# RWKV-7 chunk products: the order of the two heads of a pair on TensorE

## The chip, the cores and the metric

The kernel runs on one core of a Trainium2 chip. The metric is the device time of one execution in microseconds; the median of the runs shown for the kernel before is 1680.67 us.

## The reference

The program is one hybrid layer (sparse attention beside RWKV-7) followed by a differential-attention layer and a gated-linear-attention layer, each with a convolutional feed-forward block, on 512 tokens of width 1024 in f32. The change touches only the RWKV-7 mixer of the first layer. It has 8 heads of 64 and carries a 64x64 state per head over all tokens:

```python
def rwkv7_step(state, inp):
    r_t, w_t, k_t, v_t, kk_t, a_t = inp
    sa = jnp.einsum('bhvk,bhk->bhv', state, -kk_t)
    state = (state * w_t[:, :, None, :] + sa[..., None] * (kk_t * a_t)[:, :, None, :]
             + v_t[..., None] * k_t[:, :, None, :])
    y = jnp.einsum('bhvk,bhk->bhv', state, r_t)
    return state, y
```

Around it stand the projection with a token shift, the decays and gates, a group norm of y per head, a bonus term, a silu gate and the output projection. The kernel computes the recurrence in chunks of 64 tokens: products within a chunk, the inverse of a triangular 64x64 matrix per chunk and head, and a short chain of states over the 8 chunks.

## The kernel before, in words

Tensors are kept with features on the partitions, or with tokens on the partitions in four blocks `tb` of 128 (`NT` = 4). A block of 128 tokens holds two chunks, so `c` = 0, 1 chooses the partitions `cr` = 64c to 64c + 63. A pair of heads `f` (four pairs) shares 128 feature partitions; `hp` = 0, 1 is the head in the pair and `rows` its half, 64hp to 64hp + 63. A product `mm(out, lhsT, rhs)` on TensorE reads both operands from the same partitions (rows of the array) and writes the partitions of `out` (columns of the array). So a 64x64 product uses a quarter of the array: the row half is given by the operands' partitions, the column half by the output's.

The first phase (`phase_a`, up to some 490 us) mixes two lines of work by a written list of steps (`ORDER`): the sparse attention (steps C, K, P0 to P3, G) and the RWKV mixer. The latter is `rwkv_s1` for each pair f (steps A0 to A3), then `rwkv_inv` (I: the triangular inverses, mainly on VectorE), `rwkv_s2` (M: the six products with the inverse applied), `rwkv_chain` (H: the states over 8 chunks) and `rwkv_s5` (F: norm and gate). After both, the output projection `w_o0`. The steps are Python generators; each `yield` is where the next step of the list comes in. Weights come by DMA (`wahead`), ScalarE makes an f16 high part (`whi`) and VectorE the rest (`wlo`, line 374), always two blocks ahead, in the order of a plan.

The program is written with a tile library: it tracks which instruction reads and writes which tile, sets all waits, and writes the order in which each engine runs its instructions, with the order of the program as priority. PSUM banks have tags. The RWKV products of this phase have one bank, tag "x" (line 458, `psx()`); a product into a new `psx` tile waits until the one before it has been read. Phase A's other banks are p (2), s (3), g (1) and o (1).

The lines that matter:

- Lines 827 to 838 (`rwkv_s1`): products of 64 rows by 128 columns of output; the partitions `rows` of the head are read, and `c` chooses the column half. In the trace: `psx<-ar,sq`, `psx<-ar,sH`. Line 785, `psx<-c_u_inc,ld`: products over all 128 partitions.
- Lines 842 to 846: `psx<-sG,kT`. Here `c` chooses row half and column half together.
- Lines 848 to 861: the products that the change reorders in `rwkv_s1`, `psx<-kT,sG` and `psx<-sG,acc`. For each c, one bank takes 16 products: for the first head four blocks tb of two, then the same for the second head. ScalarE then copies the bank into Y and KV.
- Lines 946 to 970 (`rwkv_s2`): for each pair and c, 32 products into two tiles `p` and `p2`: `psx<-x,AX` (into pv; LR lies in the tile x), `psx<-Bh,AX` and `psx<-AX,Bh` (into pv2). Again first head, then second head. VectorE adds pv into R and Y, adds pv2 into KV, and makes four tiles of GT (tile lx).
- The inversion's tiles (`lx`, lines 867 to 878) come from a pool that is opened after the pool of `rwkv_s1` is closed.

Of the kernel before, what the change touches and what calls it, by code (L numbers as in the profile page):

```python
# [18 lines left out]
NT = 4  # L19
# [206 lines left out]
class Kern:  # L226
# [521 lines left out]
    def rwkv_s1(self, f):  # L748
# [51 lines left out]
        bh, kh = W("D"), W("E")  # L800
# [11 lines left out]
        khT, vT = (W(l).rearrange("p (b c) -> p b c", b=NT) for l in "AG")  # L812
        dst = [P["AX"][:, 2 * f:2 * f + 2, :, 0:64], P["Bh"][:, :, fc], khT, vT]
        for src, d, kind in ((ar[:, 0, :], dst[0], 0), (bh, dst[1], 1), (kh, dst[2], 1), (v, dst[3], 1)):
# [3 lines left out]
            if kind == 0:  # L818
                pv = p.rearrange("p (b h k) -> p b h k", b=NT, h=2)
# [6 lines left out]
        kT = self.T(sp, [128, 2, NT, 2, 64], F32, "kT")  # L826
        for hp in range(2):
            rows = slice(64 * hp, 64 * hp + 64)
# [13 lines left out]
        for hp in range(2):  # L842
            for tb in range(NT):
                for c in range(2):
                    cr = slice(64 * c, 64 * c + 64)
                    self.mm(pxv[cr, hp, tb, :], kT[cr, hp, tb, 0, :], vT[cr, tb, 64 * hp:64 * hp + 64])
        self.act(P["AX"][:, 2 * f:2 * f + 2, :, 64:128], pxv, AF.Copy)
        for c in range(2):
            cr = slice(64 * c, 64 * c + 64)
            p = self.psx()  # L850
            pv = p.rearrange("p (a b v) -> p a b v", a=2, b=NT)
            for hp in range(2):
                rows = slice(64 * hp, 64 * hp + 64)
                for tb in range(NT):
                    vv = vT[cr, tb, 64 * hp:64 * hp + 64]
                    self.mm(pv[rows, 0, tb, :], vv, kT[cr, hp, tb, 1, :])
                    self.mm(pv[rows, 1, tb, :], khT[cr, tb, 64 * hp:64 * hp + 64], vv)
            yv = P["Y"][:, f, :].rearrange("p (b c t) -> p b c t", b=NT, c=2)
            self.act(yv[:, :, c, :], pv[:, 0], AF.Copy)
            kv = P["KV"][:, f].rearrange("p (b c) v -> p b c v", b=NT)  # L860
            self.act(kv[:, :, c, :], pv[:, 1], AF.Copy)
# [66 lines left out]
    def rwkv_s2(self):  # L928
        nc, ip = self.nc, self.tp
        P, LR, Tt = self.rwt, self.rwt["LR"], self.Tt  # L930
        AXu = P["AX"].rearrange("p h b n -> p (h b) n")
        for g in range(8):
            p = self.psx()
            pv = p.rearrange("p (u n) -> p u n", u=4)
            for u in range(4):
                for c in range(2):
                    cr = slice(64 * c, 64 * c + 64)
                    self.mm(pv[cr, u, :], Tt[cr, g * 4 + u, :], AXu[cr, g * 4 + u, :])
            self.act(AXu[:, g * 4:g * 4 + 4, :], pv, AF.Copy, scale=-1.0)
            if g % 4 == 3:  # L940
                yield
        WU = P["AX"]
        id64 = self.const("id64", ip)
        GT = self.T(ip, [128, 2, 32, 32], F32, "lx").rearrange("p a b c -> p (a b c)").rearrange("p (f n k) -> p f n k", f=4, n=8)
        R, Y, KV, Bh = P["R"], P["Y"], P["KV"], P["Bh"]
        for f in range(4):
            for c in range(2):
                cr = slice(64 * c, 64 * c + 64)
                p = self.psx()
                pv = p.rearrange("p (a b t) -> p a b t", a=2, b=NT)  # L950
                p2 = self.psx()
                pv2 = p2.rearrange("p (a b t) -> p a b t", a=2, b=NT)
                for hp in range(2):
                    rows = slice(64 * hp, 64 * hp + 64)
                    h = 2 * f + hp
                    for tb in range(NT):
                        rb = LR[cr, h, tb, 1, :]
                        bh = Bh[cr, tb, h * 64:h * 64 + 64]
                        self.mm(pv[rows, 0, tb, :], WU[cr, h, tb, 0:64], rb)
                        self.mm(pv[rows, 1, tb, :], WU[cr, h, tb, 64:128], rb)  # L960
                        self.mm(pv2[rows, 0, tb, :], WU[cr, h, tb, 0:64], bh)
                        self.mm(pv2[rows, 1, tb, :], bh, WU[cr, h, tb, 64:128])
                for dst, a in ((R, 0), (Y, 1)):
                    dv = dst[:, f, :].rearrange("p (b c t) -> p b c t", b=NT, c=2)[:, :, c, :]
                    self.tt(dv, dv, pv[:, a], ALU.add)
                kv = KV[:, f].rearrange("p (b c) v -> p b c v", b=NT)[:, :, c, :]
                self.tt(kv, kv, pv2[:, 1], ALU.add)
                for tb in range(NT):
                    n = tb * 2 + c
                    self.stt(GT[:, f, n, :], id64, P["egc"][:, f, n:n + 1], pv2[:, 0, tb, :], op1=ALU.add)  # L970
            if f < 3:
                yield
        self.GT = GT
# [980 lines left out]
```

## Time and profile before

| | us |
|---|---|
| median of 3 runs | 1680.67 (1676.7 to 1681.82) |
| the profiled execution | 1679.89 |
| its span, first to last instruction | 1678.1 |
| TensorE (PE) busy | 1595.4 |
| VectorE (DVE) busy | 1040.2 |
| ScalarE (ACT) busy | 756.3 |
| GpSimd (POOL) busy | 236.5 |

The profile is of one execution. Engines: PE is TensorE's matmuls, PEld its weight loads, DVE is VectorE, ACT is ScalarE, POOL is GpSimd. A row of a group names line (often a helper's: 298 is every matmul, 285 and 288 are VectorE's helpers), engine, operation and tiles as out<-in. "x32" counts instructions. The timeline merges neighbouring instructions of one group into a row with the first start and the time to the last end; a matmul's time there holds its whole passage, so rows overlap. Waits name the engine and the work that ended them.

### The profile page before, as it was taken

The numbers are of one execution on the slowest core, as the hardware profiler recorded it, in microseconds if no ns is written. First come the engines' busy times: TensorE is split into PE (matmuls) and PEld (weight loads), VectorE is DVE, ScalarE is ACT, GpSimd is POOL, SyncE is SP. The second block draws the span as 40 slices with busy tenths as digits, with TensorE's granted clock in tenths as the row PEclk, the third lists the DMA queues.
The fourth block names the chain that finished last, engine by engine and source line by source line (L and its number), as shares of the span: only waits on it lengthen the run. The fifth ranks groups of instructions, "written<-read, shape, count | busy, mean of one in ns | idle before, by whom it ended". The sixth has DMA issues, their size and how long they took to land.

```text
span 1678.1 us, 25522 instructions
## 1 busy us (share of the span) xinstructions
PE 1595.4 (95%) x9940; PEld 853.4 (51%) x9940; DVE 1040.2 (62%) x1899; ACT 756.3 (45%) x1357; POOL 236.5 (14%) x202
## 2 busy tenths in 40 slices
PE   6999995999799998799999999999999999999999
PEld 2565562676345565444444444457664444444444
DVE  6655779777755888866777753333366477777422
ACT  4344553544654767644444432235245444444221
POOL 2200124011241011220111111101000211111000
PEclk8999998899999999999999999999899999999999
DMA  5332441434443655533333333332023333333332
GB/s 183 97 117 86 95 108 30 99 80 83 99 146 110 179 127 125 135 95 101 100 101 101 101 104 98 97 104 88 29 67 87 101 94 105 104 101 101 116 119 66
DMA packets 133817, 171.07 MB, mean 102 GB/s; under 512 B 83470, under 2 KB 95679, under 8 KB 133696
## 3 DMA queue, kind: packets, MB, share of 16 engines
q1 hardware_dynamic: 133120, 168.39, 36.1%
q8 instruction: 78, 1.28, 0.3%
q10 hardware_dynamic: 576, 1.05, 0.2%
q14 instruction: 43, 0.35, 0.1%
HBM read 137.03 MB, written 3.28 MB: 84 GB/s over the span
## 4 chain that ended last, share of the span: by engine, by line
PE 57%; DVE 3%; issue 2%; DMA 2%; ACT 1%; POOL 0%; DVEq 0%; ACTq 0%; POOLq 0%
PE psp L298 49%; PE psg L298 4%; PE pss L298 3%; PE pso L298 1%; DMA cT<-hl 1%; DMA T<-hl 1%; DVE om L285 0%; DVE wlo L285 0%; DMA wst<-in_w_o 0%; ACT whi L282 0%; ACT pe L282 0%; DVE std L1450 0%; ACT hl L282 0%; DVE hl L285 0%; DVE pss L285 0%
## 5 line engine op out<-in xcount | busy, mean ns | idle before, releaser
L298 PEld LDWEIGHTS <-whi 128*128 128x128 f16 x3508 | 337.4, 98 | 404.1 <-issue 32.3
L285 DVE SCALAR_TENSOR_TENSOR wlo<-wst,whi 128x1024 f16<-128x1024 f32 (+2 forms) x250 | 307.0, 1228 | 257.2 <-ACT whi L282 256.8
L282 ACT ACTIVATE whi<-wst 128x1024 f16<-128x1024 f32 (+2 forms) x252 | 258.2, 1025 | 401.3 <-PE psp L298 327.1
L298 PE MATMUL psp<-hh,wlo 128*128 128x512 f16 x1112 | 299.1, 386 | 17.8 <-DVE wlo L285 17.8
L298 PE MATMUL psp<-hh,whi 128*128 128x512 f16 x1112 | 297.0, 384 | 10.2 <-ACT hh L282 5.9
L298 PE MATMUL psp<-hl,whi 128*128 128x512 f16 x1112 | 293.4, 382 | 0.0
L298 PEld LDWEIGHTS <-wlo 128*128 128x128 f16 x1754 | 171.2, 99 | 218.6 <-DVE wlo L285 19.0
L285 DVE SCALAR_TENSOR_TENSOR c<-ux,vecs,c 128x511 f32<-128x511 f32 (+1 forms) x176 | 133.2, 757 | 4.9 <-ACT c L282 1.8
L288 POOL TENSOR_TENSOR gl<-gg,gh 128x512 f16<-128x512 f32 x44 | 50.9, 1157 | 423.9 <-ACT gh L282 423.9
L298 PE MATMUL psp<-gl,whi 128*128 128x512 f16 x352 | 91.6, 379 | 0.0
L298 PE MATMUL psp<-gh,wlo 128*128 128x512 f16 x352 | 91.6, 379 | 0.0
L298 PE MATMUL psp<-gh,whi 128*128 128x512 f16 x352 | 91.6, 379 | 0.0
L285 DVE SCALAR_TENSOR_TENSOR ux<-psp,rf 128x512 f32<-128x512 f32 x88 | 60.6, 688 | 32.7 <-PE psp L298 30.1
L288 POOL TENSOR_TENSOR acc<-acc,sq 128x512 f32<-128x512 f32 x34 | 53.0, 1564 | 178.4 <-ACT sq L282 178.4
L282 ACT ACTIVATE c<-ux,vecs 128x512 f32<-128x512 f32 x88 | 70.3, 798 | 1.6 <-DVE ux L285 1.6
L282 ACT ACTIVATE c<-c 128x512 f32<-128x512 f32 x44 | 27.7, 629 | 91.6 <-DVE c L285 91.6
L298 PEld LDWEIGHTS <-hh 128*128 128x128 f16 x576 | 55.9, 98 | 19.7 <-issue 4.6
L298 PE MATMUL pso<-T,vh 128*64 128x128 f16 (+1 forms) x440 | 49.3, 224 | 13.9 <-DMA T<-hl 13.1
L282 ACT ACTIVATE pss<-pss,smst 128x128 f32<-128x128 f32 (+3 forms) x64 | 32.1, 501 | 51.2 <-DVE smst L293 45.6
L298 PE MATMUL psp<-whi,hh 128*128 128x256 f16 (+3 forms) x240 | 51.6, 283 | 0.4 <-DVE kn L285 0.4
L285 DVE SCALAR_TENSOR_TENSOR gg<-c,c 128x512 f32<-128x512 f32 x44 | 30.4, 692 | 34.8 <-ACT c L282 34.8
L298 PE MATMUL psp<-whi,hl 128*128 128x256 f16 (+3 forms) x240 | 51.7, 281 | 0.0
(458 smaller groups left out, 2275.9 us busy)
## 6 DMA issues: line engine op xcount, KB each, us to landing
wst<-in_w_up SPq DMA_DIRECT2D x88, 512.0 KB, 3.5
wst<-in_w_dn SPq DMA_DIRECT2D x32, 512.0 KB, 3.5
wst<-in_w_o SPq DMA_DIRECT2D x24, 512.0 KB, 3.6
wst<-in_w_rw SPq DMA_DIRECT2D x13, 512.0 KB, 3.4
wst<-in_w_dqk SPq DMA_DIRECT2D x12, 512.0 KB, 3.8
wst<-in_w_dn SPq DMA_DIRECT2D x16, 384.0 KB, 3.1
wst<-in_w_g SPq DMA_DIRECT2D x8, 512.0 KB, 3.8
wst<-in_w_dv SPq DMA_DIRECT2D x6, 512.0 KB, 4.1
```

Source lines behind the costliest of these rows:

```text
L282: return self.nc.scalar.activation(*a, **k)
L285: return self.nc.vector.scalar_tensor_tensor(out, in0, scalar, in1, op0=op0, op1=op1)
L288: return (eng or self.nc.vector).tensor_tensor(out, a, b, op=op)
L298: return self.nc.tensor.matmul(out, lhsT=lhsT, rhs=rhs, start=start, stop=stop, **kw)
```

## The change

In both functions, the loop over the two heads becomes the innermost one, so that two successive products write the two column halves. In `rwkv_s2` the products into pv now all stand before those into pv2 in the program. Operands, outputs, number of products, evacuations and banks stay the same.

```diff
@@ rwkv_s1
-            for hp in range(2):
-                rows = slice(64 * hp, 64 * hp + 64)
-                for tb in range(NT):
-                    vv = vT[cr, tb, 64 * hp:64 * hp + 64]
-                    self.mm(pv[rows, 0, tb, :], vv, kT[cr, hp, tb, 1, :])
-                    self.mm(pv[rows, 1, tb, :], khT[cr, tb, 64 * hp:64 * hp + 64], vv)
+            halves = [(hp, slice(64 * hp, 64 * hp + 64)) for hp in range(2)]
+            for tb in range(NT):
+                for hp, rows in halves:
+                    self.mm(pv[rows, 0, tb, :], vT[cr, tb, rows], kT[cr, hp, tb, 1, :])
+                for hp, rows in halves:
+                    self.mm(pv[rows, 1, tb, :], khT[cr, tb, rows], vT[cr, tb, rows])
@@ rwkv_s2
-                for hp in range(2):
-                    rows = slice(64 * hp, 64 * hp + 64)
-                    h = 2 * f + hp
-                    for tb in range(NT):
-                        rb = LR[cr, h, tb, 1, :]
-                        bh = Bh[cr, tb, h * 64:h * 64 + 64]
-                        self.mm(pv[rows, 0, tb, :], WU[cr, h, tb, 0:64], rb)
-                        self.mm(pv[rows, 1, tb, :], WU[cr, h, tb, 64:128], rb)
-                        self.mm(pv2[rows, 0, tb, :], WU[cr, h, tb, 0:64], bh)
-                        self.mm(pv2[rows, 1, tb, :], bh, WU[cr, h, tb, 64:128])
+
+                pair = [(slice(64 * hp, 64 * hp + 64), 2 * f + hp) for hp in range(2)]
+                bh = lambda tb, h: Bh[cr, tb, h * 64:h * 64 + 64]
+                for tb in range(NT):
+                    for a in range(2):
+                        for rows, h in pair:
+                            self.mm(pv[rows, a, tb, :], WU[cr, h, tb, 64 * a:64 * a + 64], LR[cr, h, tb, 1, :])
+                for tb in range(NT):
+                    for rows, h in pair:
+                        self.mm(pv2[rows, 0, tb, :], WU[cr, h, tb, 0:64], bh(tb, h))
+                    for rows, h in pair:
+                        self.mm(pv2[rows, 1, tb, :], bh(tb, h), WU[cr, h, tb, 64:128])
```

## Rows read from the trace of the kernel before

**Rows 1.** Page part 1; table of windows: us, then busy us (instructions) per engine, PEclk

```profile
PE 1595.4 (95%) x9940; PEld 853.4 (51%) x9940; DVE 1040.2 (62%) x1899; ACT 756.3 (45%) x1357; POOL 236.5 (14%) x202
...
60.00:252.00 192.00, 182.48 (x1627) 110.29 (x1625) 121.93 (x231) 89.41 (x183) 32.89 (x28) 1.00 0.38 100
252.00:294.00 42.00, 24.09 (x124) 10.85 (x122) 41.81 (x118) 12.64 (x29) 16.91 (x13) 0.83 0.12 30
343.00:402.00 59.00, 59.00 (x766) 44.82 (x764) 40.95 (x137) 22.75 (x58) 7.47 (x6) 1.00 0.39 75
402.00:460.00 58.00, 47.31 (x456) 26.23 (x454) 45.20 (x110) 35.48 (x74) 14.23 (x11) 1.00 0.41 89
```

**Rows 2.** Instructions by tile: count, ns min/median/max, first to last start us, forms

```profile
L298 PE MATMUL psx<-kT,sG x128: 218/218/267, 99.2 to 251.0; 64*64 64x64 f32 x128
L298 PE MATMUL psx<-sG,acc x128: 218/218/218, 99.3 to 251.1; 64*64 64x64 f32 x128
L298 PEld LDWEIGHTS psx<-x,AX x256: 129/135/135, 343.4 to 397.6; 64*64 64x64 f32 x128
L298 PE MATMUL psx<-x,AX x256: 218/218/268, 343.4 to 397.6; 64*64 64x64 f32 x128
L298 PE MATMUL psx<-Bh,AX x128: 218/218/267, 346.5 to 400.5; 64*64 64x64 f32 x128
L298 PE MATMUL psx<-AX,Bh x128: 218/218/218, 346.6 to 400.6; 64*64 64x64 f32 x128
```

**Rows 3.** Timeline of TensorE, blocks of the edited lines: start us, length us

```profile
249.43 0.33 PE L298 MATMUL psx<-kT,sG 64*64 64x64 f32 x2
...
251.05 0.28 PE L298 MATMUL psx<-sG,acc 64*64 64x64 f32 x2
...
364.42 1.90 PE L298 MATMUL psx<-x,AX 64*64 64x64 f32 x32
...
367.57 0.33 PE L298 MATMUL psx<-Bh,AX 64*64 64x64 f32 x2
367.74 0.28 PE L298 MATMUL psx<-AX,Bh 64*64 64x64 f32 x2
367.86 0.28 PE L298 MATMUL psx<-Bh,AX 64*64 64x64 f32 x2
...
368.32 0.33 PE L298 MATMUL psx<-Bh,AX 64*64 64x64 f32 x4
...
369.19 0.28 PE L298 MATMUL psx<-AX,Bh 64*64 64x64 f32 x2
```

**Rows 4.** Timeline of TensorE, products of lines 846, 834 and 785

```profile
144.77 1.15 PE L298 MATMUL psx<-sG,kT 64*64 64x64 f32 x32
...
135.84 1.09 PE L298 MATMUL psx<-ar,sq 64*64 64x128 f32 x16
...
119.84 1.05 PE L298 MATMUL psx<-c_u_inc,ld 128*128 128x128 f32 x8
```

**Rows 5.** VectorE's waits, 343 to 402 us: us in total, times, longest us

```profile
DVE R L288 <- PE psx L298: 11.0, 7, 2.7
DVE KV L288 <- PE psx L298: 4.4, 7, 1.1
```

**Rows 6.** Start of the inversion and TensorE's wait in it: waits and timelines

```profile
POOL lx L877 <- PE psx L298: 2.5, 1, 2.5
...
251.37 1.97 DVE L876 STREAM_TRANSPOSE lx<-x 32x1024 f32<-32x1024 f32 x1
...
294.37 1.03 PE L298 MATMUL psp<-hh,wlo 128*128 128x512 f16 x2 [17.53 <-DVE wlo L285]
```

**Rows 7.** Instructions by tile: start of the state chain, end of R and of attention

```profile
L298 PE MATMUL psx<-KV,lx x16: 218/218/267, 403.1 to 403.6; 64*64 64x64 f32 x16
L288 POOL TENSOR_TENSOR R<-Y,R x4: 1151/1154/1162, 435.7 to 451.7; 128x512 f16<-128x512 f32 x4
L288 POOL TENSOR_TENSOR mn<-t,mn x4: 1152/1168/1600, 243.8 to 443.3; 128x512 f16<-128x512 f32 x4
```

## The prediction

> **What bounds the kernel now.** I read the page's busy shares first, then a table of windows over the first phase, where the edited lines run, then the edited products one by one, and last who waits for them. TensorE is busy 95% of the span, and in the phase's windows it leads everywhere but in one: 182.48 of 192 us from 60 to 252, all 59.00 from 343 to 402; only from 252 to 294 VectorE has 41.81 of 42 us, and there TensorE idles [rows 1]. So a microsecond of TensorE saved before 252 or between 343 and 402 should come off the time, one saved between 252 and 294 should not.
>
> The edited products are small. Each 64x64 product in f32 shows as two matmuls (the 64 products of line 959 give 128). In rwkv_s1 there are 128 + 128 matmuls, between 99.2 and 251.1 us; in rwkv_s2 256 into pv and 128 + 128 into pv2, between 343.4 and 400.6 [rows 2]. They come in blocks of 32: eight in s1 (four pairs of heads, two halves c) and sixteen in s2 (as many times a block for pv and one for pv2), 768 matmuls in all. In s2 the program writes pv and pv2 products alternately, but the trace has all 32 of pv first and those of pv2 a good microsecond later: the tile library writes the order on each engine, and pv2 waits for the one "x" bank. A block is the same everywhere: 1.90 us from first start to last end, the last matmul's own 0.22 included [rows 2], in s1 (249.43 to 251.33) and in s2 (from 364.42, and 367.57 to 369.47) [rows 3]. 1.68 us over 31 steps are 54 ns a matmul. In the middle, where the first head ends and the second begins, the view merges four matmuls in 0.33 us where it elsewhere has two in 0.28: at the one change of column half the two heads already run beside each other.
>
> **What the change does to a block.** It removes and adds no instruction, no DMA and no wait that the source names; it puts the two heads' products in turn, so that the column half changes after each product instead of once a block. The new order runs nowhere in the kernel before, so I bound the new block by its nearest relatives. From below: line 846, same shape, 32 matmuls, two tiles in turn, takes 1.15 us, so 0.93 from first to last start [rows 4]. There row half and column half change together. The change keeps the row half (both heads read partitions cr) and changes columns only, and for that the nearest row is line 834: rows fixed by the head, columns alternating with c, 16 matmuls of 128 columns in 1.09 us. Eight matmuls of 128 columns that use the whole array, and so follow one another, take 1.05. Two column halves over the same rows thus go through in the time of one. From above: no overlap at all, 31 x 58.5 ns, which is 1.81 us (58.5 is 0.117 us from one pair of matmuls to the next [rows 3], halved), 0.13 worse than now. I take 0.93, because line 834 is the same arrangement and only its width differs.
>
> Here a rule speaks against the change. What the rows show is given above: sixteen matmuls over one row half in 1.09 us [rows 4]. The Trainium skill, "TensorE: Matmul & The Clock Gate", section Part 3 on packing small matmuls, says that a weight load overlaps matmuls in flight only when the row group differs; here it does not differ. By that rule the pairs would gain nothing and the sum below would be zero; by the rows it is 0.75 us a block. The trace disagrees with the rule already in the kernel before: within one head, on the same rows, a load of 135 ns comes every 58.5 ns [rows 2, 3].
>
> **The sum.** 1.68 - 0.93 = 0.75 us a block, 24 blocks, 18.0 us of TensorE. What of it is on the path:
>
> *rwkv_s2, sixteen blocks, 12.0 us.* TensorE is full from 343 to 402, and VectorE waits for it: the add into R waits for the pv block 11.0 us in 7 cases (1.57 each), the add into KV for the pv2 block 4.4 us in 7 (0.63 each) [rows 5]. So the R side has cover for the whole 0.75; on the KV side VectorE would be the late one after 0.63. That makes 8 x (0.75 + 0.63), 11.0 us. VectorE holds 40.95 of 59 us there [rows 1]; over 48 us that is 85%, tight and still under full. Between blocks TensorE does attention and projection work while the bank is emptied; that work and its gaps stay as they are.
>
> *rwkv_s1, eight blocks, 6.0 us.* They lie before the inversion, where TensorE is 95% busy. All eight gate it, the last two as well: the inversion's tiles take the memory that s1's tiles leave, its memset on GpSimd waits 2.5 us for a psx product, and its first transpose on VectorE starts at 251.37, just as the last block ends at 251.33 [rows 3, 6]. But VectorE has attention work up to that moment too, and chains on ScalarE and VectorE hold TensorE for the other 5%. I count three quarters, 4.5 us; if nothing of it reached the inversion, which VectorE bounds by itself, it would be 0, and TensorE would only stand longer than the 17.53 us that it stands there now [rows 6].
>
> *What comes after.* The end of s2 releases the state chain, four head-pair epilogues and the output projection. R is finished (all heads) by 452.9 us, the attention heads by 444.5 [rows 7]: the RWKV side is last, by 8.4 us, so attention becomes the late one only if RWKV comes forward by more than that against it. RWKV would come forward by 15.5, and attention by less, since part of its work is on VectorE (45.20 of 58 us from 402 to 460). TensorE has 10.7 us of idle time in that window to close up [rows 1]. I take off 1.6 for this, an estimate between nothing and the 7.1 us that would be lost if attention did not move at all.
>
> Sum: 11.0 + 4.5 - 1.6 = 13.9 us. The profiled execution took 1679.89 us (span 1678.1 and 1.8 around it), 0.8 under the median of 1680.67. On the median: 1666.8.
>
> **Rivals.** *The blocks shrink but the time is handed back.* In s2 the one bank is emptied by VectorE, which runs its instructions in order between attention's; if its queue becomes the limit, or attention does after 444, some 8 us are lost and 6 are left: 1674.7. For it speaks VectorE's 45.20 of 58 us after 402; against it the 15.4 us that it waits for these very blocks.
>
> *The pairs do not overlap.* Two heads read the same rows, and each product might wait for the other head's. Then nothing is gained, and by the upper bound 24 x 0.13, or 3 us, could be lost: 1680.7 to 1684. Line 834 speaks against it. This is also what the Trainium skill's section above would give.
>
> *Slower, by a new order.* The library orders every engine's instructions anew, and a faster block moves all that follows. The place that can hurt is the inversion: VectorE's queue is full from 252 to 294, and one weight split behind it held TensorE for 17.53 us [rows 6]. TensorE did 24.09 us of work there before it stood [rows 1]. If an earlier split falls behind the inversion's steps, up to those 24 us move into stretches where TensorE is full. It decides from 13.9 us on; at 19, halfway between that and 24, it gives 1686. Against it: the split order follows the weight plan, which the change does not touch, and the inversion begins after attention work that is not edited.
>
> **How the numbers follow.** The forecast, 9 to 18 us gained, has 0.68; time handed back 0.15 (two thirds of it still over the bound below); no overlap 0.05; a new order 0.12, of which 0.10 measurably slower. About 0.3%, 5 us, is what a measurement of this kernel can tell from no change. Faster: 0.68 + 0.10 = 0.78. Same: 0.05 + 0.05 + 0.02 = 0.12. Slower: 0.10. The range runs from 1660, all 18.0 us with 2.7 us more from a luckier order, to 1680, the handed-back case whole and the start of no change.
>
> **What would show it.** Right: a block of 32 in the edited lines takes about 1.15 us instead of 1.90; the state chain starts about 15 us earlier than 403.1; the add into KV hardly waits for TensorE any more and the add into R about half as long. Wrong in the first step: blocks still near 1.9 us. Wrong in the second: short blocks, but gaps between them longer than the 1.25 us between the blocks at 364.42 and 367.57, with VectorE as what they wait for. Wrong by order: a TensorE wait for a weight split longer than 17.5 us, or a second one.

## The result, and the profile after

The changed kernel took 1660.8 us (median of 4 runs, 1657.63 to 1665.93) against 1680.55 for the kernel before (4 runs, 1676.7 to 1681.82): a ratio of 0.9891 [0.9855, 0.9926], 19.8 us less. Longer series followed with the experiments, and in them the gain is smaller: 1663.76 (11 runs) and 1663.82 (8 runs) against 1676.03 (34 runs) and 1676.55 (19 runs) of the kernel before on the same chips, so 12.3 and 12.7 us, ratios 0.9919 [0.9891, 0.9947] and 0.9932 [0.9899, 0.9965]. One of the 85 later runs of the kernel before, at 1713.67 us with a granted clock of 0.931, lay in a slower state and is left out throughout. I take 12 to 13 us as the size of the gain. Where the other 7 us of the first result came from is a question of its own, taken up below.

The two programs' instructions, engine by engine and in order, are the same on VectorE, ScalarE, GpSimd and SyncE; on TensorE they differ only inside the blocks of the edited lines.

The page's first part and a table of windows of the changed kernel, cut at the same places of the work as [rows 1]: us, busy us and instructions of PE, PEld, DVE, ACT and POOL, granted clock, DMA share, GB/s.

```profile
PE 1570.5 (95%) x9940; PEld 832.1 (50%) x9940; DVE 1040.0 (63%) x1899; ACT 756.1 (46%) x1357; POOL 238.3 (14%) x202
...
60.00:247.00 187.00, 175.54 (x1619) 103.67 (x1616) 120.00 (x227) 88.27 (x181) 32.28 (x27) 1.00 0.39 102
247.00:290.50 43.50, 25.05 (x133) 11.27 (x127) 43.21 (x122) 13.17 (x30) 17.52 (x13) 0.83 0.13 32
341.00:391.00 50.00, 47.12 (x765) 33.00 (x764) 41.14 (x136) 22.39 (x57) 7.41 (x6) 1.00 0.49 87
391.00:449.00 58.00, 47.17 (x455) 26.16 (x454) 45.28 (x110) 35.54 (x74) 14.02 (x11) 1.00 0.42 90
```

The third window is rwkv_s2: 59 us in [rows 1] with TensorE full, 50 now, and TensorE has 2.88 us of idle time in it. The window behind it is as long as before, instruction counts and busy times too.

TensorE's timeline of the changed kernel, blocks of the edited lines in rwkv_s2: start, length, and in brackets the idle time before a row and what ended it.

```profile
341.28 1.15 PE L298 MATMUL psx<-x,AX 64*64 64x64 f32 x32
...
344.31 0.33 PE L298 MATMUL psx<-Bh,AX 64*64 64x64 f32 x4 [0.70 <-DVE Y L288]
344.44 0.31 PE L298 MATMUL psx<-AX,Bh 64*64 64x64 f32 x4
...
364.76 1.15 PE L298 MATMUL psx<-x,AX 64*64 64x64 f32 x32 [0.21 <-DVE lx L285]
366.78 0.48 PE L298 MATMUL pss<-kd,qr 128*128 128x384 f16 x2 [0.88 <-DVE smst L293]
...
367.90 0.33 PE L298 MATMUL psx<-Bh,AX 64*64 64x64 f32 x4
...
369.28 0.22 PE L298 MATMUL pso<-T,vh 128*64 128x128 f16 x1 [0.23 <-DMA T<-hl]
...
375.93 0.22 PE L298 MATMUL pso<-T,vh 128*64 128x128 f16 x1 [0.87 <-DMA T<-hl]
```

A block of 32 takes 1.15 us where [rows 3] has 1.90, which is 0.93 from first to last start instead of 1.68, exactly the lower bound taken from line 846 [rows 4]. All 24 edited blocks, those of rwkv_s1 too, take 0.93 in the trace. All matmuls now come in the merged form, four in 0.28 to 0.33 us, that [rows 3] shows only at the one change of column half. A single matmul is no faster (218 ns, as in [rows 2]): twice as many start in the same time.

Waits of the changed kernel from 341 to 391 us: us in total, times, longest.

```profile
DVE R L288 <- PE psx L298: 4.6, 6, 1.7
...
PE pso L298 <- DMA T<-hl: 1.1, 2, 0.9
...
PE pss L298 <- DVE smst L293: 0.9, 1, 0.9
...
PE psx L298 <- DVE Y L288: 0.7, 1, 0.7
...
DVE KV L288 <- PE psx L298: 0.3, 1, 0.3
```

VectorE's wait for pv fell from 11.0 to 4.6 us and the one for pv2 from 4.4 to 0.3 [rows 5]. In their place TensorE waits, which it did not do here before.

Instructions by tile of the changed kernel, the marks of [rows 6] and [rows 7]: count, ns min/median/max, first to last start.

```profile
L876 DVE STREAM_TRANSPOSE lx<-x x4: 1935/1966/1973, 248.0 to 256.1; 32x1024 f32<-32x1024 f32 x4
...
L298 PE MATMUL psx<-KV,lx x16: 218/218/267, 392.1 to 392.6; 64*64 64x64 f32 x16
...
L288 POOL TENSOR_TENSOR R<-Y,R x4: 1152/1154/1157, 425.0 to 440.9; 128x512 f16<-128x512 f32 x4
...
L288 POOL TENSOR_TENSOR mn<-t,mn x4: 1155/1167/1600, 240.5 to 432.5; 128x512 f16<-128x512 f32 x4
```

The inversion starts at 248.0 instead of 251.4, the state chain at 392.1 instead of 403.1; R and attention (mn) both end 10.8 us earlier than in [rows 7]. So the profiled pair divides as follows, each stretch as the distance of two such marks:

```
stretch                                       before    after   gained
start to the inversion's first transpose       251.4    248.0      3.4
inversion on VectorE, to its end in line 895    51.5     51.5      0.0
from there to the first pv block of s2          40.5     41.8     -1.3
first pv to last pv2 block of s2                57.4     48.6      8.8
from there to the last w_o product of R         87.2     87.3     -0.1
everything after                              1190.1   1178.7     11.4
span                                          1678.1   1655.9     22.2
```

Half of what this pair shows lies in the last stretch, in which the two programs are the same. The 1.3 us lost ahead of s2 go with the clock: that stretch has 13.7 us at 1.2 GHz in the changed kernel's execution and 6.8 in the other, and a second execution of the kernel before, with 13.7, takes 42.5 us for it.

### The profile page after: what moved, and what is told of

Same layout as the page of the kernel before. It is cut to its first block, busy times and chain, and to the rows that moved or that the text cites. A ratio compares the mean times of both kernels' runs of the same rounds, so it can differ in the third digit from the quotient of the medians.

```text
span 1655.9 us, 25522 instructions
## 1 busy us (share of the span) xinstructions
PE 1570.5 (95%) x9940; PEld 832.1 (50%) x9940; DVE 1040.0 (63%) x1899; ACT 756.1 (46%) x1357; POOL 238.3 (14%) x202
## 4 chain that ended last, share of the span: by engine, by line
PE 57%; DVE 3%; DMA 2%; issue 2%; ACT 1%; POOL 0%; SPq 0%; DVEq 0%; ACTq 0%; POOLq 0%
PE psp L298 50%; PE psg L298 4%; PE pss L298 3%; PE pso L298 1%; DMA cT<-hl 1%; DMA T<-hl 0%; DVE om L285 0%; ACT pe L282 0%; DVE wlo L285 0%; DVE std L1452 0%; DVE pss L285 0%; DVE hl L285 0%; DMA m<-in_memT 0%; DVE pe L293 0%; DMA wst<-in_w_mk 0%
## 5 line engine op out<-in xcount | busy, mean ns | idle before, releaser
L285 DVE SCALAR_TENSOR_TENSOR ux<-psp,rf 128x512 f32<-128x512 f32 x88 | 60.6, 688 | 32.7 <-PE psp L298 30.2
L298 PE MATMUL pso<-T,vh 128*64 128x128 f16 (+1 forms) x440 | 49.0, 224 | 14.6 <-DMA T<-hl 13.7
L282 ACT ACTIVATE pss<-pss,smst 128x128 f32<-128x128 f32 (+3 forms) x64 | 32.1, 501 | 48.8 <-DVE smst L293 44.7
```

Of the source, the lines that this page charges most:

```text
L282: return self.nc.scalar.activation(*a, **k)
L285: return self.nc.vector.scalar_tensor_tensor(out, in0, scalar, in1, op0=op0, op1=op1)
L298: return self.nc.tensor.matmul(out, lhsT=lhsT, rhs=rhs, start=start, stop=stop, **kw)
```

## The experiments

**Each half alone, and both kernels again.** s1_only keeps the change in rwkv_s1 and takes it back in rwkv_s2, s2_only the other way round; the two repeats are the unchanged files. The edits, shortened:

```diff
 # s1_only, in rwkv_s2 (the order of before)
+for hp in range(2):
+    for tb in range(NT):
+        mm(pv 0); mm(pv 1); mm(pv2 0); mm(pv2 1)
 # s2_only, in rwkv_s1 (the order of before)
+for hp in range(2):
+    for tb in range(NT):
+        mm(pv 0); mm(pv 1)
```

> The kernel before, unchanged, profiled a second time. Theory A (the gain lies in the first phase, about 11 us, and what was gained after it is the TensorE clock, which is granted anew in each execution): first phase ends (last read of R by w_o) again at 488 +- 2 us; the rest takes 1190 us only if the granted clock there has again some 48 us at its lower level; with 20 us less of them it takes 10 us less, so the times of the runs should scatter by several us with the clock. Theory B (the part after the first phase is slower for this kernel by its own schedule): the rest takes 1190 +- 1 us again, whatever the clock.

> The changed kernel, unchanged, profiled a second time. Theory A: first phase ends at 477 +- 3 us again; the rest takes between 1178 and 1190 us, by 0.5 us for each us of the lower clock level, so it can come out as long as in the kernel before. Theory B: the rest takes 1179 +- 1 us again.

> Only the s1 products take the new order. My forecast gave this part 4.5 of its 6.0 us. Theory A: blocks of 0.93 us in s1, 1.68 in s2; the inversion begins some 3.4 us earlier (248 instead of 251.4) and the phase ends 3 to 4 us earlier than in the kernel before, 484 to 485; in time 0.998 of it. Rival (s1 is hidden by the inversion on VectorE): the phase ends at 488, ratio 1.000.

> Only the s2 products take the new order. My forecast gave this part 11.0 of its 12.0 us. Theory A: s2 ends 9 to 11 us earlier against the inversion's end and the phase ends at 477 to 479; ratio 0.993 to 0.995. Rival (VectorE's emptying of the one bank takes over): s2 shortens by less than 6 us, ratio above 0.996.

Medians on one chip, 11 to 12 runs each, ratios to the 34 runs of before at 1676.03: before again 1676.45, 0.9997 [0.9973, 1.002]; after again 1663.76, 0.9919 [0.9891, 0.9947]; s1 alone 1675.45, 0.9988 [0.9965, 1.0012]; s2 alone 1668.52, 0.9951 [0.993, 0.9972].

By its median s1 alone is worth nothing that can be told apart, and s2 some 7.5 us. But the marks say otherwise for s1. By tile, s1 alone:

```profile
L876 DVE STREAM_TRANSPOSE lx<-x x4: 1924/1965/1979, 246.3 to 254.5; 32x1024 f32<-32x1024 f32 x4
...
L298 PE MATMUL psx<-KV,lx x16: 218/218/267, 398.2 to 398.6; 64*64 64x64 f32 x16
```

and s2 alone:

```profile
L876 DVE STREAM_TRANSPOSE lx<-x x4: 1944/1957/1967, 250.7 to 258.8; 32x1024 f32<-32x1024 f32 x4
...
L298 PE MATMUL psx<-KV,lx x16: 218/218/267, 393.9 to 394.3; 64*64 64x64 f32 x16
```

With s1 alone the inversion begins 5.1 us before 251.4 and the chain 4.9 us before 403.1, and s2 is as long as before (57.4); with s2 alone the inversion begins where it did (0.7 off, as far off as in before again) and the chain 9.2 us earlier. The two halves act at their own places and don't touch each other. At the end of the edited phase, the last w_o product of R, s1 alone keeps only part of its 5 us: that comes at 488.0 and 487.3 us in the two executions of the kernel before, at 485.3 with s1 alone and at 478.7 with s2 alone. With both it comes at 477.2, 474.9 and 475.0 in the three executions of the changed kernel, 10 to 13 us earlier than before, and what the clock does afterwards has no part in this. That the median of s1 alone does not show even the 2 to 3 us left is put down to the clock below, by a fitted line.

**What the clock does to these times.** Each run lists its mean granted clock (1 is all the time at 2.4 GHz, 0.5 all at 1.2). Within the runs of every kernel the time rises by 1.1 to 1.6 us for each 0.001 that this falls (correlations of 0.81 to 0.97). The profiles show where: two executions of the changed kernel, after and after again, over the stretch behind the edited phase and then over the first GLA recurrence in it (same columns as the windows above). After:

```profile
1167.50:1186.60 19.10, 19.10 (x111) 13.02 (x110) 5.02 (x12) 0.78 (x3) 0.79 (x2) 1.00 0.08 27
...
477.00:1655.00 1178.00, 1151.90 (x6067) 591.95 (x6065) 705.88 (x1142) 527.51 (x889) 135.69 (x114) 0.99 0.36 104
```

After again:

```profile
1141.40:1168.90 27.50, 27.50 (x288) 24.04 (x286) 11.87 (x19) 11.16 (x21) 1.22 (x1) 1.00 0.24 78
1168.90:1199.10 30.20, 30.20 (x111) 19.93 (x110) 4.99 (x12) 0.74 (x3) 1.05 (x2) 0.57 0.06 18
...
475.00:1670.00 1195.00, 1167.97 (x6066) 603.59 (x6065) 706.24 (x1142) 527.77 (x889) 134.55 (x114) 0.97 0.34 102
```

The same 111 matmuls take 19.1 us at 1.00 and 30.2 at 0.57, right behind 27.5 us with TensorE full at 1.00; the whole rest takes 1178 us in one execution and 1195 in the other. Over the first ten profiles of this study (both kernels, each half, both run lengths, inversion_too and GLA_too) the length of that rest goes with the time at 1.2 GHz in it, 23.9 to 64.9 us, as 1169.7 + 0.37 us for each (correlation 0.96). A later profile, after_third, took 1186.6 with 47.8 us of it, where the line gives 1187.4. The profiled execution of before had 47.8 us of it and that of after 28.7, which by that line is 7.1 of the 11.4 us in the table's last row; the line's scatter of some 3 us at either end can hold the remainder. The first result was too good on both sides: its four runs of after had a median clock of 0.976, against 0.972 in the 19 later ones, and its four of before, at 1680.55, lay 4 us over the median of the 84 later ones.

So I put a line through each kernel's own runs and read it at one clock, 0.973. The copy of the kernel before comes out 1.3 us from the kernel before, and the two repeats of after 1.9 apart; so far these figures can be trusted, and no further.

```
kernel              runs   median    median clock   at clock 0.973   gained
before (3 chips)      84   1676.6       0.974            1677.6
before again          12   1676.45      0.973            1676.3          1.3
after, twice          19   1663.8       0.972            1663.8         13.8
s1 alone              12   1675.45      0.9715           1672.9          4.7
s2 alone              12   1668.52      0.9735           1668.2          9.4
runs of 2             10   1667.92      0.9715           1665.8         11.8
runs of 4             10   1669.37      0.973            1669.8          7.8
inversion too          9   1668.05      0.972            1666.5         11.1
GLA too               10   1668.58      0.969            1663.2         14.4
both too              12   1669.42      0.9685           1664.7         12.9
```

At one clock s1 and s2 alone add up to 14.1, and the whole change gives 13.8. Such a reading is fair only where the change itself leaves the clock alone, which does not hold for the two GLA rows (below).

**How often the column half must change.** The overlap could need a change after every product, or a few products in a row could do as well; and if the gain came from anything but the overlap, the run length would not matter. Runs of 2 and of 4 products on a head before the other head follows (the change has runs of 1, the kernel before of 8), in s1 and s2; s1's edit, shortened:

```diff
-for tb in range(NT):
-    for hp, rows in halves:
-        mm(pv 0, tb)
-    for hp, rows in halves:
-        mm(pv 1, tb)
+for t0 in range(0, NT, 1):          # runs of 4: step 2, and tb in t0, t0 + 1
+    for hp, rows in halves:
+        for tb in range(t0, t0 + 1):
+            mm(pv 0, tb); mm(pv 1, tb)
```

> The changed kernel, but each head has two products in a row before the other head's turn. In the kernel before, a head has eight in a row and a block starts its last matmul 1.68 us after the first; without any overlap that would be 1.81, so one change of head hid 0.13 us. Theory A (a change of column half lets about two products of the waiting head run beside the last two of the other, whatever the length of the run): seven changes hide 0.9 us, a block is 0.9 to 1.0 us as in the changed kernel, phase end 475 to 478, ratio 0.991 to 0.994. Rival (only strict alternation overlaps): block 1.3 us or more, ratio above 0.995.

> As before with four products of a head in a row: three changes of head in a block. Theory A: 1.81 - 3 x 0.13 = 1.42 us a block, so about a third of the gain: the first phase ends 4 to 5 us earlier than in the kernel before, 483 to 484; ratio 0.996 to 0.998. Rival (the engine looks further ahead): block near 0.93. Rival (strict alternation alone): block 1.68.

Medians 1667.92 (10 runs), 0.9939 [0.9912, 0.9965], and 1669.37 (10 runs), 0.9962 [0.9942, 0.9982]; from here on ratios are to the runs of before on the same chip. The first pv block of s2 in TensorE's timeline, runs of 2:

```profile
341.36 1.20 PE L298 MATMUL psx<-x,AX 64*64 64x64 f32 x32
```

runs of 4:

```profile
342.98 1.54 PE L298 MATMUL psx<-x,AX 64*64 64x64 f32 x32
```

From first to last start that is 0.93, 0.98, 1.32 and 1.68 us for runs of 1, 2, 4 and 8 products. Without any overlap it would be 1.81 (31 times 58.5 ns, the prediction's upper bound). So one change saves 0.13 us in the kernel before, three save 0.49 (0.16 each), seven save 0.83 (0.12 each), and fifteen 0.88, where the floor is reached: both halves full all the time. A change of half thus hides some two to three matmuls of 58.5 ns, one to one and a half products, and no more. Runs of 4 were expected at 1.42 and came out 1.32: each change was worth a little more than the one in [rows 3] had shown. The time follows the block (7.8 us gained with blocks at 1.32, 11.8 at 0.98, 13.8 at 0.93, at one clock). So does s2 in the profiles, from its first block to its last, in executions that have no time at 1.2 GHz there: 57.4 us with runs of 8, 52.0 with 4, 48.6 with 2, and 48.5 to 48.8 with 1. And so the overlap is shown to be the cause.

**The same order elsewhere.** The inversion's two rounds of 32x32 products (lines 908 and 920) and the GLA recurrence use other parts of the array one after another too. In inversion_too the two diagonal halves c alternate after each product; in GLA_too the products of two heads that use different column halves alternate; both_too has both. after_third is the changed kernel beside it. The edits, shortened:

```diff
 # inversion_too, both rounds
-for c in range(2):
-    for u in range(16):
-        matmul(pv[b, u], ...)
+for u in range(16):
+    for c in range(2):
+        matmul(pv[b, u], ...)
 # GLA_too, inside a step of the recurrence
-for e in range(2):
-    for part in parts[e]: mm(o, vt, sct); mm(o, st[e], qe)
-    state update of e
+part 0 of e=0; then part 1 of e=0 and part 0 of e=1, product by product
+state update of e=0; part 1 of e=1; state update of e=1
```

> The changed kernel, and in the inversion's four blocks of 64 matmuls (32x32, lines 908 and 920) the two chunks c, which use different row and column quarters, are taken in turn instead of sixteen products of the one and then sixteen of the other. Theory A (products in different parts of the array run beside each other): a block of 2.11 us goes to about 1.1 to 1.3 us, four of them on the path between the inversion on VectorE and s2, so s2 starts 3 to 4.5 us earlier and the time falls by 3 to 4 us against the changed kernel, if the order of the other work, which does change here, costs nothing. Rival (32 columns are too short: each matmul already takes the least time that there is between two starts): blocks stay at 2.1 us, no change.

> The changed kernel, and in the gated-linear-attention recurrence the products of the two heads of a pair that write the two halves of one block (64 columns each) are taken in turn. Theory A: 16 pairs of matmuls of 128 columns (each 0.19 us apart now) and 28 of 64 columns (0.1 us apart) give back half of their time, some 3 + 2 us in the two stretches of 26 us in which TensorE leads; time 2 to 4 us below the changed kernel. Rival (these loads have 96 or 128 rows and do not overlap, or the state's chain over VectorE sets the step): no change within 1 us in those stretches.

> The changed kernel with both further reorderings, the inversion's blocks and the gated-linear-attention pairs. From the single runs: s2 ends some 6 us earlier, but the first phase ends no earlier (476.6 before, since attention is then late), and the two recurrences take 1 us less each at equal clock. Theory: time within 3 us of the changed kernel in this call, ratio 0.990 to 0.994; the inversion's gain is handed back before 477. Rival (the handing back was the clock of that one profile, 6.8 us at the lower level): phase end at 471 to 473 and a ratio of 0.986 to 0.989.

> The changed kernel once more, as the mark for the run beside it. First phase ends at 475 to 478; ratio 0.990 to 0.994; the rest takes 1170 us and 0.37 us for each us at the lower clock level, as in the ten profiles so far (1178 to 1195).

inversion_too 1668.05 (9 runs), 0.9937 [0.9914, 0.9961]; GLA_too 1668.58 (10 runs), 0.9946 [0.9926, 0.9967]; both_too 1669.42 (12 runs), 0.9965 [0.9945, 0.9986]; after_third 1663.82 (8 runs), 0.9932 [0.9899, 0.9965]. None beats the changed kernel, though the inversion's products themselves got shorter; both_too, expected within 3 us of after_third beside it, came out 5.6 us above it in the median. Line 908 in the timeline of the changed kernel, 64 matmuls of 32x32, then TensorE's wait for attention in the state chain, and the chain's later products by tile:

```profile
299.56 2.11 PE L908 MATMUL psx<-itmp,x 32*32 32x32 f32 x64
...
399.51 0.52 PE L1294 MATMUL psg<-c_ident,t 128*64 128x128 f32 x3 [0.71 <-DVE t L288]
...
L298 PE MATMUL psx<-R,Z x96: 218/218/267, 396.1 to 411.3; 64*64 64x64 f32 x96
```

and in inversion_too, with its marks by tile:

```profile
298.34 1.20 PE L908 MATMUL psx<-itmp,x 32*32 32x32 f32 x64
...
395.74 0.63 PE L1294 MATMUL psg<-c_ident,t 128*64 128x128 f32 x4 [3.04 <-DVE t L288]
...
398.25 1.12 PE L298 MATMUL psx<-Z,lx 64*64 64x64 f32 x16
...
L298 PE MATMUL psx<-R,Z x96: 218/218/366, 390.7 to 411.0; 64*64 64x64 f32 x96
...
L298 PE MATMUL psx<-KV,lx x16: 218/218/267, 385.2 to 385.6; 64*64 64x64 f32 x16
...
L288 POOL TENSOR_TENSOR R<-Y,R x4: 1151/1154/1157, 425.5 to 440.2; 128x512 f16<-128x512 f32 x4
...
L288 POOL TENSOR_TENSOR mn<-t,mn x4: 1153/1156/1604, 239.4 to 431.8; 128x512 f16<-128x512 f32 x4
```

The state chain starts 6.9 us before the 392.1 of the changed kernel, but R ends only 0.7 us and attention only 0.7 us earlier: 6 us are handed back between s2 and the output projection, as the rival "handed back" had it for attention, but one step further on. They go in the state chain, which lasts from 385.2 to 411.0 us where the changed kernel's lasts from 392.1 to 411.3. TensorE stands there once for 3.04 us for attention's tile t, which VectorE has late (0.71 in the changed kernel). It goes on at 395.74, from 397.4 to 404.2 it is at 1.2 GHz, and 16 matmuls of the chain take 1.12 us instead of 0.68. The execution of both_too has both again, a wait of 3.03 us and 6.8 us at 1.2 GHz, and ends the phase at 479.3 us, after all three executions of the changed kernel. Why t is late is not settled: reordering the inversion's products also gives VectorE a new order of the work from 311 us on, attention's above all, and no run separates that from the RWKV side coming earlier.

GLA_too is level with the changed kernel at one clock (1663.2 against 1663.8), but it and both_too run at a lower clock: 0.9690 on average (10 runs) and 0.9679 (12), where the kernel before has 0.9733 (31) and 0.9734 (19) on the same two chips, and the changed kernel 0.972 (19). Single runs scatter by 0.003, so chance hardly does this; what the two kernels share and the others lack is the order of the GLA products. Whether it is the denser products that bring the clock down these runs don't tell, nor how much shorter the GLA's products got: in both profiles its two recurrences were in part at 1.2 GHz.

**A shorter emptying of the bank.** Is it VectorE's work on the one bank that keeps s2 from giving its full 12 us? The four multiply-adds that follow a pv2 block become one addition; this leaves out the decay factor egc in GT.

```diff
-for tb in range(NT):
-    n = tb * 2 + c
-    self.stt(GT[:, f, n, :], id64, P["egc"][:, f, n:n + 1], pv2[:, 0, tb, :], op1=ALU.add)
+gv = GT[:, f].rearrange("p (b c) k -> p b c k", b=NT)[:, :, c, :]
+self.tt(gv, pv2[:, 0], id64[:, None, :].to_broadcast([128, NT, 64]), ALU.add)
```

> The changed kernel with the four multiply-adds that empty the state factors out of the bank (0.85 us for a pair and half) replaced by one add of 256 columns (about 0.42 us); left out is the decay factor in them. The question is what holds s2 at 48.7 us, when the shorter blocks alone would give 57.4 - 12.0 = 45.4. Theory (VectorE's emptying of the one bank is the limit): eight times 0.43 us, s2 takes 45 to 46 us. Rival (attention's chain, its softmax on VectorE and ScalarE and its transposes by DMA, which TensorE's fixed order waits for): s2 stays at 48 to 49 us, or the order changes and it shortens by less than 1.5.

One run, 1676.8 at a clock of 0.964, beside 1676.55 for 19 runs of before. Its window over s2, the timeline's rows with a wait there, and VectorE's work into lx (GT) by line, the changed kernel's last:

```profile
341.00:390.00 49.00, 46.44 (x721) 33.63 (x720) 34.47 (x108) 20.96 (x55) 6.45 (x6) 0.86 0.42 77
...
344.16 0.33 PE L298 MATMUL psx<-Bh,AX 64*64 64x64 f32 x4 [0.70 <-DVE Y L288]
357.90 0.22 PE L298 MATMUL pso<-T,vh 128*64 128x128 f16 x1 [1.86 <-DMA T<-hl]
...
L288 DVE TENSOR_TENSOR lx<-psx,c_id 128x256 f32<-128x256 f32 x8 | 3.3, 416 | 0.0
...
L285 DVE SCALAR_TENSOR_TENSOR lx<-c_id,egc,psx 128x64 f32<-128x64 f32 x32 | 6.8, 273 | 0.0
```

The edit takes 3.5 us of work from VectorE, and s2 is no shorter (49.0 against 48.6), with TensorE still idle for 2.56 us. But this execution was at 1.2 GHz for 13.7 us inside s2, where all others were at full clock, and four of its sixteen blocks, at 1.30 to 1.66 us instead of 0.93, alone took 2.3 us longer by it. The edit also changed the order in which VectorE and TensorE do attention's work. So the length proves nothing. What stands is that the wait for Y is untouched, and that the larger part of TensorE's idle time is again for attention's tile T. Its total can't be read for the question. The profiles answer part of it elsewhere: in inversion_too and both_too the emptying is as in the changed kernel and attention's work stands in another order, and s2 takes 45.9 and 46.2 us, all at 2.4 GHz. So the emptying alone does not hold it at 48.6.

## Why the prediction was right

The forecast was 1666.8 us with 13.9 gained; measured were 1660.8 in the first series and 1663.8 in the longer ones, which is 12.3 and 12.7 us gained, or 13.8 at one clock. The sum came out, but two of its terms were off, one by 2.2 us too much and one by 1.6 too little: that they nearly made up for each other is luck.

*The block, 1.68 to 0.93: right to the hundredth.* Line 834, same rows and alternating columns, was the right relative. The Trainium skill, "TensorE: Matmul & The Clock Gate", Part 3 on packing small matmuls, has a weight load overlap running matmuls only when the row group differs. The trace disagrees: here only the column half changes, and 32 matmuls take 1.15 us instead of 1.90.

*rwkv_s1, 4.5 us: right.* The inversion begins 3.4 us earlier in the profiled pair and 5.1 with s1 alone; at one clock s1 alone gives 4.7, within the 1 to 2 us by which such figures differ, and at the end of the phase it keeps 2 to 3. The inversion itself did not change (51.5 us), nor did TensorE's wait for the weight split in it: 17.56 us, against 17.53 in [rows 6].

*rwkv_s2, 11.0 us: mis-sized, 8.7 to 8.8.* The sixteen blocks gave their 12.0 us (16 times 0.75), but the stretch shrank from 57.4 to 48.6: the gaps between the blocks grew by 3.1, of which 2.88 are TensorE's own idle time in the window from 341 to 391. The prediction looked for the loss on the KV side of the emptying (8 times 0.12). Read from the waits, the emptying took little: 0.70 us once for Y, on the R side, behind an attention multiply of 1.19 us on VectorE, and 0.21 for lx, on the KV side. The other 2.0 us are attention's, 0.88 for its statistic smst and 1.1 for its transposed tile T: these had hidden behind the longer blocks. So the "work between blocks that stays as it is" was the part that did not. This is read from the trace; the experiment meant to prove it was spoilt by the clock, but the 45.9 us of inversion_too, with the emptying as it was, fit it.

*After s2, -1.6 us: not seen.* Attention moved forward with RWKV, both by 10.8 us, and the stretch from s2 to the end of the phase is 87.2 us before and 87.3 after. VectorE and TensorE are as busy there as before [rows 1], only earlier. A loss does appear once s2 ends earlier still (inversion_too).

*The signs.* Of those for being right, the blocks and VectorE's two waits came as told; the state chain starts 11.0 us earlier in the pair and 12 to 13 in the other two executions, not 15. One sign of being wrong in the second step came too: two of the eight gaps from pv to pv2 grew past 1.25 us, from 1.14 to 1.88 and from 1.06 to 1.99, with VectorE as what TensorE waited for.

*The rivals.* "The pairs do not overlap" is refuted by the blocks; "a new order" by the instruction lists and the 17.56 us; "handed back" came true in part, 3.1 us inside s2 instead of 8, and in full only for the further step in inversion_too. What no rival had was the clock: single runs of one kernel moved with it by more than 10 us (1659.16 to 1672.0 for the changed kernel), more than the forecast's own error.

## What to carry to other kernels

Where small products use one half of the array's columns and another head's products use the other, write them in turn, one product each: over 32 matmuls it gave almost a factor of two, and runs of up to two products kept most of it. Price such a change by the stretch in which TensorE is full, and then look at what other chains between the blocks had been hidden behind the longer ones. And when a kernel's runs differ in granted clock, compare them at one clock, or over some ten runs: four of each made 12.5 us look like 19.8.

## What was not expected of the hardware

Behind the edited phase the time at 1.2 GHz lay between 23.9 and 64.9 us from execution to execution, over instructions that are the same in all but the GLA variants, and between 28.7 and 64.9 for the changed kernel alone; by the fitted line each microsecond of it went with 0.37 us. TensorE shows as busy throughout in both clocks, so the busy share does not tell: the same 111 matmuls of a recurrence take 19.1 us or 30.2. With the GLA products in turn the mean granted clock was lower, 0.969 and 0.968 against 0.973. The change of column half hides two to three matmuls at the seam and no more, so a longer run on one half is not made up later.
